# The last product of the down phase in two column halves, in a hybrid encoder layer on one Trainium2 core

## The chip, the core and the metric

The kernel runs on one core of a Trainium2 chip as one launch. A core has a matrix engine (TensorE, PE in the profile, with its weight loads as PEld), a vector engine (VectorE, DVE), a scalar engine (ScalarE, ACT), a general engine (GpSimd, POOL) and a queue that mostly issues transfers (SyncE, SP). Each works through its own instructions in order; semaphores order work between engines. Working memory on the core is SBUF, and matrix products land in PSUM, which here is handed out as tiles of 128 partitions x 512 fp32 values, eight of them, in two rings of four (`mm` and `hy`). Arrays live in HBM and move by DMA.

The metric is the device time of one execution, in microseconds (us), as the median over runs.

## The reference, cut to what matters

The layer has a convolution and recurrence stage, an attention stage and a feed-forward stage; only the last one and the final norm matter here:

```
def _rms_norm(x, g):
    xf = x.astype(jnp.float32)
    y = xf * lax.rsqrt(jnp.mean(xf * xf, axis=-1, keepdims=True) + EPS)
    return (y * g.astype(jnp.float32)).astype(x.dtype)
...
        h = h + jnp.square(jax.nn.relu(_rms_norm(h, norm_ff_g[l]) @ ff_w1[l])) @ ff_w2[l]
    return _rms_norm(h, final_norm_g)
```

There is one such layer. `h` has 2048 rows of 1024 columns, `ff_w1` is 1024 x 4096 and `ff_w2` 4096 x 1024, all in fp32. A row's root needs the squares of all its 1024 columns, so the two column halves of a row come together before it can be scaled and stored.

## The kernel before, in words

**Products in three passes.** An fp32 operand is split into a high and a low part (`halves`, L1622 and L1623, or L365), and `mm3` makes a product of three matmuls: high x high (L354), high x low (L357), low x high (L358). A "pass" below is one such matmul instruction.

**The down phase.** The second matrix product of the feed-forward stage is made by a Strassen-like scheme of 2 x 2 blocks: seven products `i` in the order `ORDER_DOWN = (1, 6, 7, 5, 3, 2, 4)` for each quarter `o` of the 4096 inner columns, 28 products in all. Each product is made for two groups `tp` of 512 activation rows, and over four steps `k` of 128 inner values. One step is four blocks `m` of 128 columns of the product's output times three passes of 512 columns (the 512 rows of the group: the result lies transposed, output features on partitions). After step `k == 3` the four PSUM tiles (`bank[m]`, from the ring `mm` for `tp` 0 and `hy` for `tp` 1) are added to accumulators `acc[i, tp]` in SBUF by DVE (L1949).

**The way out.** When a quarter-block of the result is complete, it is turned back: `turn` (L1879) makes four transposes of 128 x 128 on TensorE (L1882) into one PSUM tile, takes the sum of squares on ACT (L1884) into `ss`, and multiplies the tile by the final gain on DVE (L1885). `finish(c, dst)` (L1887) does the rest for 512 rows `c`: on DVE the mean of squares of both column halves (`mo`, L1891), a root by nine more small instructions after a first guess (`rsqrt`, L229 to L233), then scaling by the root, for even `c` the right column half on DVE (L1897) and the left half on ACT (L1899), and a store after every second block of 128 rows (L1902; 256 rows x 512 columns, 512 KB; the right half on SP's queue, the left half on ACT's). The functions wait in a list `outs`, from which the step loop takes one or two after each step's passes, and what is left is run after the loop. The last product (number 27, `i` = 4, `tp` = 1) completes rows 1024 to 1535 (`c` = 2). While it is made, the list holds the four turns and the `finish` of rows 0 to 511 (`c` = 0), whose last block was completed by the product just before.

**What sets the order.** The framework decides the order of the instructions on each engine when the program is built, by a simulated timeline, taking what was traced first where several are ready. It also places all semaphores. `keep_in_program_order` pins one instruction behind whatever was traced last before it on its engine; in this part it is used for the four adds of the last product alone (L1951).

Of the kernel before, what the change touches and what calls it, by code (L numbers as in the profile page):

```python
# [10 lines left out]
F32 = mybir.dt.float32  # L11
# [3 lines left out]
ALU = mybir.AluOpType  # L15
# [5 lines left out]
D = 1024  # L21
# [112 lines left out]
class Prog:  # L134
# [1592 lines left out]
    def ffn(self):  # L1727
        nc, tc, a = self.nc, self.tc, self.a
# [4 lines left out]
        prods = [(o, i) for o in range(4) for i in self.ORDER_DOWN]  # L1733
        down = [(n, tp, k) for n in range(len(prods)) for tp in range(2) for k in range(4)]
        aq, bq = {}, {}
# [37 lines left out]
        with tc.tile_pool(name="up", bufs=1) as U:  # L1773
# [25 lines left out]
            us, cs = {}, {}  # L1799
            for n, (tp, g, i) in enumerate(steps):  # L1800
# [13 lines left out]
                if n + 2 >= len(steps):  # L1814
                    k = n + 2 - len(steps)
# [4 lines left out]
                bank = self.ffn_product(wq.pop(0), i) if n > 1 else self.first[n]  # L1820
                u, c = us.setdefault(g, {}), cs.setdefault(g, {})
# [14 lines left out]
                else:  # L1836
# [5 lines left out]
                    t = [self.stage() for _ in range(4)]  # L1842
# [12 lines left out]
        with tc.tile_pool(name="down", bufs=1) as B:  # L1855
            acc, ms = {}, []
            on = [B.tile([128, D], F32, tag="on", name="on", bufs=2) for _ in range(2)]
            for tp in range(2):
                for h in range(2):
                    v = on[tp][:, 512 * h:512 * h + 512]  # L1860
# [8 lines left out]
            def residual(i, tp, k):  # L1869
                n, h = {2: (0, 0), 7: (1, 1), 3: (1, 0), 4: (0, 1)}[i]  # L1870
                v = acc[i, tp][:, k]
                nc.sync.dma_start(out=v, in_=h2[2 * tp + n, :, 4 * h + k])
                nc.gpsimd.tensor_tensor(v, v, ms[2 * tp + n], ALU.mult)
                if i == 4:
                    nc.gpsimd.tensor_tensor(v, v, acc[7, tp][:, k], ALU.subtract)

            ss = B.tile([128, 4, 2, 4], F32, name="ss")

            def turn(c, h, src, dst, t, tag):  # L1879
                pt = self.ps.tile([128, 512], F32, tag=tag, name=tag, bufs=4)  # L1880
                for k in range(4):
                    nc.tensor.transpose(pt[:, 128 * k:128 * k + 128], src[:, k, 128 * t:128 * t + 128], self.ident)  # L1882
                junk = B.tile([128, 512], F32, tag="junk", name="junk", bufs=1)
                nc.scalar.activation(junk, pt, AF.Square, accum_out=ss[:, c, h, t:t + 1])  # L1884
                nc.vector.tensor_tensor(dst[:, t], pt, gl[:, 512 * h:512 * h + 512], ALU.mult)  # L1885

            def finish(c, dst):  # L1887
                m = B.tile([128, 4], F32, tag="mo", name="mo", bufs=2)
                q = self.rbp[:, 4 * c:4 * c + 4]
                for h in range(2):  # L1890
                    nc.vector.scalar_tensor_tensor(m, ss[:, c, h], 1.0 / D, m if h else q, ALU.mult, ALU.add)  # L1891
                rv = self.rsqrt(B, m, "or")
                for t in range(4):
                    for h in range(2):
                        v = dst[h][:, t]
                        if h and c % 2 == 0:
                            nc.vector.tensor_scalar(v, v, rv[:, t:t + 1], None, ALU.mult)  # L1897
                        else:
                            nc.scalar.mul(v, v, rv[:, t:t + 1])  # L1899
                        if t % 2:  # L1900
                            r0 = 512 * c + 128 * (t - 1)
                            (nc.sync if h and c % 2 == 0 else nc.scalar).dma_start(  # L1902
                                out=self.out[r0:r0 + 256, 512 * h:512 * h + 512].rearrange("(t p) c -> p t c", p=128),
                                in_=dst[h][:, t - 1:t + 1])
# [8 lines left out]
            def add(i, j, tp, eng):  # L1913
                for m in range(4):
                    eng.tensor_tensor(acc[i, tp][:, m], acc[i, tp][:, m], acc[j, tp][:, m], ALU.add)

            early = [(i, tp, k) for i in (7, 4, 3, 2) for tp in range(2) for k in range(4)]
            outs = []
            V, G = nc.vector, nc.gpsimd
            for s, (n, tp, k) in enumerate(down):  # L1920
                o, i = prods[n]
                if n == 0 and tp == 0:
                    sums_w(k, nc.vector.tensor_tensor)
                if s + 3 < len(down):
                    fetch_b(s + 3, G if s > 199 and k else V)
                if o < 3 and tp == 0 and i == 2:
                    load_w(o + 1, k)
                if o < 3 and tp == 0 and i == 4:
                    sums_w(k, late=True)
                if early and (3 < s < 20 or s > 19 and s % 3):  # L1930
                    residual(*early.pop(0))
                if k == 0:
                    bank = [self.hy() if tp else self.mm() for _ in range(4)]
                (ah, al), (bh, bl) = aq[n, k], bq.pop(s)
                for m in range(4):
                    msl = slice(128 * m, 128 * m + 128)
                    self.mm3(bank[m], ah[:, msl], al[:, msl], bh, bl, k == 0, k == 3)
                if tp and n + 1 < len(prods):
                    fetch_a(n + 1, k)
                for _ in range(min(len(outs), 2 if len(outs) > 4 or n + 1 == len(prods) else 1)):  # L1940
                    outs.pop(0)("mm" if tp else "hy")
                if k < 3:
                    continue
                for m in range(4):
                    v = acc[i, tp][:, m]
                    if o == 0 and i in (1, 6, 5):
                        nc.scalar.copy(v, bank[m])
                    else:
                        d = nc.vector.tensor_tensor(v, bank[m], v, ALU.add)  # L1949
                        if s + 1 == len(down):  # L1950
                            tc.keep_in_program_order(d)  # L1951
                if o < 3:
                    continue
                if i == 1:
                    add(2, 1, tp, G)
                elif i == 6:
                    add(6, 1, tp, V)
                elif i == 7:
                    add(7, 6, tp, V)
                    add(3, 6, tp, G)  # L1960
                elif i == 5:
                    add(3, 5, tp, V)
                    add(5, 7, tp, G)
                    add(4, 7, tp, G)
                    if tp:
                        outs += turned(1, 0, 1, 5, 1)
                elif i == 3:
                    c = 2 * tp + 1
                    if not tp:
                        outs += turned(3, 1, 1, 5, 1)  # L1970
                    outs += turned(c, tp, 0, 3, 6, (acc[6, tp], acc[1, tp]))
                elif i == 2:
                    outs += turned(2 * tp, tp, 0, 2, 7)
                elif i == 4:
                    outs += turned(2 * tp, tp, 1, 4, 5, (acc[7, tp], acc[5, tp]))
            for x in outs:
                x("mm")


TC_ARGS = dict(schedule_with_timeline_sim=True)  # L1980
# [123 lines left out]
```

## Time and profile before

| | |
|---|---|
| three runs | 3126.7, 3130.87 and 3132.18 us, median 3130.87 |
| profiled execution | 3127.22 us, its span 3125.4 us |
| granted clock of TensorE over the span | 0.987 of full speed |
| busy share of the span | PE 97%, DVE 63%, ACT 48%, POOL 37% |
| the last product, from its first pass to the start of its last | 3094.96 to 3107.43 us |
| busy from 3100 us to the end, in us of 26 | PE 10.26, DVE 14.67, ACT 10.63 |
| last store issued | 3119.37 us |

The span runs from the first to the last instruction of the profiled execution. A timeline row gives start, duration, engine, line of the kernel, operation, output and inputs with their sizes, the count of instructions merged in it and, in brackets, how long the engine had stood idle and which instruction released it. A matmul's duration includes its way through the array; the next one starts before it ends, so its price is the distance of two starts.

### The profile page before, as it was taken

How to read it: one execution, taken by the hardware profiler on the slowest of the kernel's cores; microseconds unless marked ns; L12 is line 12 of the kernel's file. 1: busy time of each engine (PE TensorE's matmuls, PEld its weight loads, DVE VectorE, ACT ScalarE, POOL GpSimd, SP SyncE). 2: the span in 40 equal slices, each digit the busy share in tenths (PEclk: the TensorE clock that was granted, in tenths of full speed). 3: DMA queues.
4: the chain of work that ended last, by engine and by line, in shares of the span. 5: the costliest groups of instructions: out<-in, count | busy, mean ns of one | idle time of the engine just before them, and what ended most of it. 6: DMA issues, size and time to landing. Idle time of an engine off the chain costs nothing.

```text
span 3125.4 us, 42916 instructions
## 1 busy us (share of the span) xinstructions
PE 3031.2 (97%) x14257; PEld 2377.4 (76%) x14257; DVE 1960.3 (63%) x3448; ACT 1487.1 (48%) x2907; POOL 1146.5 (37%) x802
## 2 busy tenths in 40 slices
PE   8999999989999898999999999999999999999998
PEld 6655667766677666888888888888888888888876
DVE  7965466446646455777765556557555686565695
ACT  5443366533656225555544455556555443333335
POOL 0122012200113343324141327776565475242693
PEclk9999999999999998999999999999999999999999
DMA  6564767676877897455385647656644565353524
GB/s 211 153 212 163 235 204 220 192 217 217 240 207 246 267 315 242 142 184 197 115 280 175 226 154 246 207 187 219 213 151 150 167 216 187 111 165 112 161 91 172
DMA packets 444101, 607.07 MB, mean 194 GB/s; under 512 B 38494, under 2 KB 248542, under 8 KB 442856
## 3 DMA queue, kind: packets, MB, share of 16 engines
q1 hardware_dynamic: 405988, 546.54, 54.5%
q10 hardware_dynamic: 37892, 57.79, 5.4%
q8 instruction: 113, 1.85, 0.2%
q14 instruction: 108, 0.88, 0.1%
HBM read 401.79 MB, written 202.41 MB: 193 GB/s over the span
## 4 chain that ended last, share of the span: by engine, by line
PE 84%; DMA 6%; DVE 4%; ACT 2%; issue 2%; POOL 1%; SPq 0%; ACTq 0%; DVEq 0%; POOLq 0%
PE mm L354 17%; PE mm L358 17%; PE mm L357 17%; PE hy L358 6%; PE hy L354 6%; PE hy L357 6%; PE hy L177 3%; PE mm L912 2%; PE hy L943 2%; PE hy L985 1%; DMA a<-hy 1%; PE hy L1279 1%; PE mm L674 1%; PE mm L703 1%; PE hy L1281 1%
## 5 line engine op out<-in xcount | busy, mean ns | idle before, releaser
L1623 DVE TENSOR_TENSOR bl<-wr,bh 128x512 fp32r<-128x512 f32 x213 | 240.3, 1134 | 129.9 <-ACT bh L1622 129.7
L1622 ACT CAST ah<-w 128x512 fp32r<-128x512 f32 x284 | 176.6, 623 | 301.5 <-PE hy L357 155.2
L365 DVE TENSOR_TENSOR wl<-wn,wh 128x512 fp32r<-128x512 f32 (+1 forms) x300 | 218.1, 773 | 99.9 <-ACT wh L365 99.4
L354 PE MATMUL mm<-xh,wh 128*128 128x512 f32 x640 | 267.5, 419 | 12.1 <-ACT wh L365 9.1
L990 POOL TENSOR_TENSOR b<-b,a 128x512 f32<-128x512 f32 x64 | 87.4, 1367 | 509.3 <-ACT b L988 214.5
L357 PE MATMUL mm<-xl,wh 128*128 128x512 f32 x640 | 255.6, 399 | 0.7 <-DVE xl L365 0.6
L358 PE MATMUL mm<-xh,wl 128*128 128x512 f32 x640 | 254.8, 399 | 0.0
L1622 ACT CAST bh<-wr 128x512 fp32r<-128x512 f32 x232 | 143.5, 621 | 229.1 <-PE mm L358 177.0
L1623 DVE TENSOR_TENSOR al<-w,ah 128x512 fp32r<-128x512 f32 x236 | 216.7, 918 | 55.4 <-ACT ah L1622 55.2
L358 PE MATMUL mm<-bh,al 128*128 128x512 f32 x576 | 224.0, 391 | 2.6 <-POOL al L1623 2.6
L354 PE MATMUL mm<-bh,ah 128*128 128x512 f32 x576 | 225.9, 392 | 0.4 <-DVE acc L1785 0.3
L357 PE MATMUL mm<-bl,ah 128*128 128x512 f32 x576 | 224.9, 390 | 0.0
L365 ACT CAST wh<-wn 128x512 fp32r<-128x512 f32 (+1 forms) x300 | 166.6, 618 | 113.8 <-PE mm L358 51.4
L357 PE MATMUL mm<-act,wh 128*128 128x512 f32 x512 | 200.5, 393 | 0.8 <-DVE act L365 0.8
L354 PE MATMUL mm<-act,wh 128*128 128x512 f32 x512 | 198.8, 394 | 2.5 <-ACT wh L365 2.4
L358 PE MATMUL mm<-act,wl 128*128 128x512 f32 x512 | 199.1, 392 | 0.0
L354 PE MATMUL hy<-bh,ah 128*128 128x512 f32 x448 | 175.2, 391 | 0.0
L357 PE MATMUL hy<-bl,ah 128*128 128x512 f32 x448 | 174.6, 390 | 0.0
L358 PE MATMUL hy<-bh,al 128*128 128x512 f32 x448 | 174.4, 390 | 0.0
L354 PEld LDWEIGHTS mm<-xh,wh 128*128 128x128 f32 x640 | 121.3, 190 | 67.2 <-issue 19.0
L354 PE MATMUL mm<-wh,xh 128*128 128x256 f32 (+1 forms) x512 | 155.9, 305 | 10.6 <-ACT xh L365 8.1
L336 POOL TENSOR_TENSOR b<-b 128x512 f32<-128x512 f32 x32 | 58.3, 1822 | 277.4 <-DVE b L333 137.6
(369 smaller groups left out, 8282.3 us busy)
## 6 DMA issues: line engine op xcount, KB each, us to landing
wr<-hc SPq DMA_DIRECT2D x224, 256.0 KB
w<-in_ff_w_dram SPq DMA_DIRECT2D x172, 256.0 KB
hc<-wn SPq DMA_DIRECT2D x128, 256.0 KB
wn<-in_w_in_dram SPq DMA_DIRECT2D x100, 256.0 KB
hc<-q SPq DMA_DIRECT2D x96, 256.0 KB
fs<-a SPq DMA_DIRECT2D x32, 512.0 KB
a<-fs SPq DMA_DIRECT2D x64, 256.0 KB
a<-zs SPq DMA_DIRECT2D x64, 256.0 KB
```

Source lines behind the costliest of these rows:

```text
L177: b = self.nc.tensor.matmul(*products[-1], start=True, stop=True)
L336: nc.gpsimd.tensor_tensor(e[1], f, b, ALU.subtract)
L354: first = mm(ps, lh, rh, start=start, stop=False)
L357: mm(ps, lh, rl, start=False, stop=False)
L358: self.last = mm(ps, ll, rh, start=False, stop=stop)
L365: both = (self.nc.scalar.copy(hi, src), self.nc.vector.tensor_tensor(lo, src, hi.bitcast(F32), ALU.subtract))
L674: mul(p[:, m], w[:, k, ms], mt[k // 4][:, k % 4], start=k == 0, stop=k == 7)
L912: nc.tensor.matmul(pp, dm[:, m], t[:, m], start=True, stop=True)
L943: nc.tensor.matmul(pg, em[:, m], y, start=True, stop=True)
L990: nc.gpsimd.tensor_tensor(xt, xt, hi[:, m], ALU.mult)
L1622: self.nc.scalar.copy(hi, src)
L1623: eng.tensor_tensor(lo, src, hi.bitcast(F32), ALU.subtract)
```

## The change

The last product for `tp` = 1 leaves the step loop and is made by a new function, `last_block`: twice the four steps, first for the columns 0 to 255 of the four PSUM tiles (activation rows 1024 to 1279), then for the columns 256 to 511 (rows 1280 to 1535) of the same four tiles. After each half, four adds of 256 columns bring it to the accumulator, each pinned in program order, and two turns and a `finish` for these two blocks of 128 rows go on the list. `finish` gets a range of blocks for that. In the first half two entries of the list are taken after each step; in the second half none after step 0 and one after each later step. What is left is run at the end.

```diff
@@ -1884,19 +1884,20 @@
                 nc.scalar.activation(junk, pt, AF.Square, accum_out=ss[:, c, h, t:t + 1])
                 nc.vector.tensor_tensor(dst[:, t], pt, gl[:, 512 * h:512 * h + 512], ALU.mult)
 
-            def finish(c, dst):
-                m = B.tile([128, 4], F32, tag="mo", name="mo", bufs=2)
-                q = self.rbp[:, 4 * c:4 * c + 4]
+            def finish(c, dst, ts=range(4)):
+                m = B.tile([128, 4], F32, tag="mo", name="mo", bufs=2)[:, 0:len(ts)]
+                t0 = ts[0]
+                q = self.rbp[:, 4 * c + t0:4 * c + t0 + len(ts)]
                 for h in range(2):
-                    nc.vector.scalar_tensor_tensor(m, ss[:, c, h], 1.0 / D, m if h else q, ALU.mult, ALU.add)
+                    nc.vector.scalar_tensor_tensor(m, ss[:, c, h, t0:t0 + len(ts)], 1.0 / D, m if h else q, ALU.mult, ALU.add)
                 rv = self.rsqrt(B, m, "or")
-                for t in range(4):
+                for t in ts:
                     for h in range(2):
                         v = dst[h][:, t]
                         if h and c % 2 == 0:
-                            nc.vector.tensor_scalar(v, v, rv[:, t:t + 1], None, ALU.mult)
+                            nc.vector.tensor_scalar(v, v, rv[:, t - t0:t - t0 + 1], None, ALU.mult)
                         else:
-                            nc.scalar.mul(v, v, rv[:, t:t + 1])
+                            nc.scalar.mul(v, v, rv[:, t - t0:t - t0 + 1])
                         if t % 2:
                             r0 = 512 * c + 128 * (t - 1)
                             (nc.sync if h and c % 2 == 0 else nc.scalar).dma_start(
@@ -1913,6 +1914,28 @@
             def add(i, j, tp, eng):
                 for m in range(4):
                     eng.tensor_tensor(acc[i, tp][:, m], acc[i, tp][:, m], acc[j, tp][:, m], ALU.add)
+
+            def last_block(i, tp):
+                n = len(prods) - 1
+                bank = [self.hy() for _ in range(4)]
+                for half in range(2):
+                    cs = slice(256 * half, 256 * half + 256)
+                    for k in range(4):
+                        (ah, al), (bh, bl) = aq[n, k], bq[len(down) - 4 + k]
+                        for m in range(4):
+                            msl = slice(128 * m, 128 * m + 128)
+                            self.mm3(bank[m][:, cs], ah[:, msl], al[:, msl], bh[:, cs], bl[:, cs], k == 0, k == 3)
+                        for _ in range(min(len(outs), 1 if half and k else 0 if half else 2)):
+                            outs.pop(0)("mm")
+                    for m in range(4):
+                        v = acc[i, tp][:, m, cs]
+                        tc.keep_in_program_order(nc.vector.tensor_tensor(v, bank[m][:, cs], v, ALU.add))
+                    c = 2 * tp
+                    for t in (2 * half, 2 * half + 1):
+                        outs.append(lambda tag, t=t: turn(c, tp, acc[i, tp], acc[5, tp], t, tag))
+                    outs.append(lambda tag, half=half: finish(c, (acc[7, tp], acc[5, tp]), range(2 * half, 2 * half + 2)))
+                for x in outs:
+                    x("mm")
 
             early = [(i, tp, k) for i in (7, 4, 3, 2) for tp in range(2) for k in range(4)]
             outs = []
@@ -1929,6 +1952,10 @@
                     sums_w(k, late=True)
                 if early and (3 < s < 20 or s > 19 and s % 3):
                     residual(*early.pop(0))
+                if s + 4 >= len(down):
+                    if k == 3:
+                        last_block(i, tp)
+                    continue
                 if k == 0:
                     bank = [self.hy() if tp else self.mm() for _ in range(4)]
                 (ah, al), (bh, bl) = aq[n, k], bq.pop(s)
@@ -1946,9 +1973,7 @@
                     if o == 0 and i in (1, 6, 5):
                         nc.scalar.copy(v, bank[m])
                     else:
-                        d = nc.vector.tensor_tensor(v, bank[m], v, ALU.add)
-                        if s + 1 == len(down):
-                            tc.keep_in_program_order(d)
+                        nc.vector.tensor_tensor(v, bank[m], v, ALU.add)
                 if o < 3:
                     continue
                 if i == 1:
@@ -1973,8 +1998,6 @@
                     outs += turned(2 * tp, tp, 0, 2, 7)
                 elif i == 4:
                     outs += turned(2 * tp, tp, 1, 4, 5, (acc[7, tp], acc[5, tp]))
-            for x in outs:
-                x("mm")
 
 
 TC_ARGS = dict(schedule_with_timeline_sim=True)
```

## The prediction

> **What bounds the kernel now.** I read the head of the page and its chain first, then the same chain cut to the last 30 us, then the timeline of that stretch on all engines.
>
> ```profile
> span 3125.4 us, 42916 instructions
> PE 84%; DMA 6%; DVE 4%; ACT 2%; issue 2%; POOL 1%; SPq 0%; ACTq 0%; DVEq 0%; POOLq 0%
> ```
> ```profile
> 3106.65 1.67 DVE acc L1897 x4
> 3108.32 0.61 DVE acc L1949
> 3108.97 2.14 PE mm L1882 x13
> ```
>
> TensorE bounds the kernel as a whole, but not its end. The chain near the end runs over DVE: the four scalings of `finish(0)` (L1897; it norms rows 0 to 511 of the output), then the adds of the last product (L1949), then its transposes. The change touches only the last 31 us, so the timeline of these gives the rest (start, duration, engine, line):
>
> ```profile
> 3094.96 0.39 PE L354 MATMUL hy<-bh,ah 128*128 128x512 f32 x1
> ...
> 3099.50 0.28 PE L1882 MATMUL mm<-ident,acc 128*128 128x128 f32 x1
> ...
> 3101.30 1.04 PE L1882 MATMUL mm<-ident,acc 128*128 128x128 f32 x8
> ...
> 3101.71 2.85 DVE L1885 TENSOR_TENSOR acc<-mm,gl 128x512 f32<-128x512 f32 x4 [4.30 <-ACT junk L1884]
> ...
> 3104.03 0.39 PE L358 MATMUL hy<-bh,al 128*128 128x512 f32 x1
> ...
> 3106.65 1.67 DVE L1897 TENSOR_SCALAR acc<-acc,or_y 128x512 f32<-128x512 f32 x4
> ...
> 3107.43 0.39 PE L358 MATMUL hy<-bh,al 128*128 128x512 f32 x1
> ...
> 3108.24 2.48 DVE L1949 TENSOR_TENSOR acc<-hy,acc 128x512 f32<-128x512 f32 x4
> ...
> 3108.97 2.45 PE L1882 MATMUL mm<-ident,acc 128*128 128x128 f32 x16 [1.16 <-DVE acc L1949]
> ...
> 3110.77 0.42 PEld L1882 LDWEIGHTS mm<-ident,acc 128*128 128x128 f32 x4 [0.18 <-DVE acc L1949]
> 3111.14 0.60 ACT L1884 ACTIVATE junk<-mm 128x512 f32<-128x512 f32 x1 [1.92 <-PE mm L1882]
> ...
> 3111.86 2.85 DVE L1885 TENSOR_TENSOR acc<-mm,gl 128x512 f32<-128x512 f32 x4 [1.14 <-ACT junk L1884]
> ...
> 3113.30 0.60 ACT L1884 ACTIVATE junk<-mm 128x512 f32<-128x512 f32 x1
> ...
> 3114.62 0.15 DVE L1891 SCALAR_TENSOR_TENSOR mo<-ss,mo 128x4 f32<-128x4 f32 x1
> ...
> 3116.78 1.67 DVE L1897 TENSOR_SCALAR acc<-acc,or_y 128x512 f32<-128x512 f32 x4
> ...
> 3118.14 0.38 ACTq L1902 DMA_DIRECT2D out_dram<-acc  x1
> ...
> 3119.37 0.38 ACTq L1902 DMA_DIRECT2D out_dram<-acc  x1
> ```
>
> The last pass starts at 3107.43, but DVE is inside `finish(0)` from 3101.71 to 3108.24: that, not TensorE, starts the last chain. Four adds, sixteen transposes, four squares, four gains, the root (3114.62 to 3116.78, 2.16 us of 4-column instructions), scalings, stores.
>
> **The change, part by part.** *Passes.* 48 passes of 512 columns become 96 of 256. From 3104.03 to 3107.43 lie 15 steps of 512 columns, 0.227 us each. For 256 columns:
>
> ```profile
> 1029.85 0.28 PE L354 MATMUL mm<-wh,xh 128*128 128x256 f32 x1
> ...
> 1032.96 0.28 PE L358 MATMUL mm<-wh,xl 128*128 128x256 f32 x1
> ```
>
> 26 steps in 3.11 us, 0.120 each, with a weight load before each of them as in the new passes. So 96 x 0.120 - 48 x 0.227 = +0.6 us of TensorE. A transpose paces at (1.04 - 0.27) / 7 = 0.11 (the row at 3101.30). The first half is 48 x 0.120 + 16 x 0.11 (the four turns of rows 0 to 511, popped after its steps 0 and 1) = 7.5 us: from 3094.96 to 3102.5. The same sum for the old block, 47 x 0.227 + 16 x 0.11 = 12.4, meets its 3107.43 - 3094.96.
>
> *What the tail counts.* Transposes, squares, gains, scalings (16, 4, 4, 8) and stores (4, two on SP's queue with those of rows 0 to 511, two on ACT's) stay as many; the adds become 8 of half the width; a second `mo` pair and root (12 instructions at 0.2 us) are added. A store's issue holds ACT 0.38 us, as before.
>
> *Where the first half's adds go.* They are pinned behind whatever was traced last on DVE, and that is the last L1897 of `finish(0)`; the old adds had the same pin and started at 3108.24 on its heels. The transposes of `finish(0)` stood after 20 passes (3099.50); as 40 half passes that is 4.8 in place of 4.5 us, so +0.25: the adds start at 3108.5. Bounds: -0.5 if they come some passes earlier, +0.8 if later. Nothing covers this: DVE is busy until then.
>
> *A wait for the bank.* Both halves of one block write the same PSUM tile, columns 0-255 and 256-511. Does a pass to the second columns wait for an add that reads the first? No row shows that pair; the nearest is a tile whose columns 0-255 ACT reads and whose columns 256-271 DVE reads:
>
> ```profile
> 513.72 0.38 ACT L851 ACTIVATE st<-mm 128x256 f32<-128x256 f32 x1
> 514.14 0.18 DVE L856 TENSOR_TENSOR sg<-mm,par 128x16 f32<-128x16 f32 x1 [1.16 <-ACT st L851]
> ...
>   ACT st L851: 18.9, 9
> ```
>
> DVE had no datum to wait for and still stood 18.9 us in 9 waits until ACT left the tile. So access is ordered by tile, not by column, and I take the wait as there: TensorE stands from 3102.5 until the first add is done. Behind the waiting pass on TensorE's queue are all passes of the second half and, between them, the transposes of the first half's turns; for those wait ACT's squares, DVE's gains and the first half's root. The price lies between 0 (columns apart, passes start at 3102.5) and 6.5 us of standing. The Trainium skill (PSUM — Partial Sum Buffer, "PSUM bank collisions raise a hardware error") says the same of writes: two engines on one bank collide whichever columns they touch, so software keeps them apart by bank; the trace agrees for two readers, and by this rule the sum is the one with the wait.
>
> An add of 256 columns has no row either. The 512-column one paces at (2.48 - 0.68) / 3 = 0.60 us; half of that, 0.30, is the floor, 0.60 the ceiling. A copy of 258 columns from PSUM:
>
> ```profile
> L1156 DVE COPY cb<-hy 128x258 f32<-128x258 f32 x2 | 0.8, 422 | 0.0
> ```
>
> I take 0.43 for one and a pace of 0.36. The passes restart at 3108.5 + 0.43 + 0.05 = 3109.0; the other three banks come free in time (three passes take 0.36).
>
> *The clock.* TensorE now stands over 6 us. Granted clock by the microsecond (third number from the end of a row; the first pair after the time is TensorE's busy time):
>
> ```profile
> 37.00:38.00 1.00, 0.62 (x1) 0.30 (x2) 0.33 (x2) 0.00 (x0) 0.00 (x0) 0.90 0.00 0
> ...
> 44.00:45.00 1.00, 1.00 (x4) 0.79 (x3) 0.97 (x2) 0.00 (x0) 0.00 (x0) 0.68 0.00 0
> ```
> ```profile
> 1079.72 6.44 PE L691 MATMUL mm<-kt,wm 128*128 128x256 f32 x15 [10.94 <-ACT o L681]
> ```
> ```profile
> 1085.00:1086.00 1.00, 1.00 (x4) 0.85 (x3) 0.79 (x5) 1.00 (x5) 0.00 (x0) 0.65 1.03 398
> ```
> ```profile
> 3113.00:3114.00 1.00, 0.00 (x0) 0.00 (x0) 0.96 (x2) 0.95 (x4) 0.00 (x0) 0.61 0.73 281
> ```
> ```profile
> 680.98 0.43 PE L357 MATMUL mm<-wl,xh 128*128 128x272 f32 x1
> ...
> 682.57 0.43 PE L357 MATMUL mm<-wl,xh 128*128 128x272 f32 x1
> ...
> 684.97 0.29 PE L358 MATMUL mm<-wh,xl 128*128 128x272 f32 x1
> ...
> 685.98 0.29 PE L357 MATMUL mm<-wl,xh 128*128 128x272 f32 x1
> ```
>
> The last transposes end at 3111.4 and the clock halves at 3113.2 (0.61 is 22% of 1.0 and the rest 0.5): 1.8 us of standing are enough. It comes back 5.9 us after a restart (1079.72 to 1085.7) and 7.2 us after another (37.4 to 44.6). At half clock 272 columns pace at 1.59 / 7 = 0.227, later at 1.01 / 8 = 0.126: 1.8 times. Those 5.9 and 7.2 us include breaks, the new passes have none, so I take 5.1 slow us, which cost 5.1 x (1 - 0.126 / 0.227) = 2.3; bounds 0 (no fall) and 3.2 (7.2 us). The Trainium skill (TensorE: Matmul & The Clock Gate, "What's actually happening") gives a free-running window of 3413 ns, one idle window for the fall and one busy one for the return. By 3.4 slow us the term would be 1.5, an estimate, and the sum 0.8 lower; the trace agrees on fall and return, and its returns took longer.
>
> *The first half's chain.* `turn` of block 0 is popped after the second half's step 1 and block 1 after step 2, so the second stands behind 36 passes and 8 transposes: 36 x 0.120 + 8 x 0.11 + 2.3 = 7.5 us, to 3116.5. The square starts 0.37 after the last transpose's issue (3110.77 to 3111.14), at 3116.7, gain +0.72, `mo` +0.60, root +2.16, two L1897 at (3108.24 - 3106.65) / 4 = 0.40 each: 3121.0. The last adds are pinned behind those. The passes, done by 3118.5, no longer count.
>
> *The second half's chain.* Last add starts 3 x 0.36 later, +0.43 + 0.05 + 0.37 to the first square, 3122.9; at half clock (TensorE stood 3 us again) +0.2: 3123.1. Second square, its gain, `mo`, root: 0.72 + 0.72 + 0.60 + 2.16: the root is ready at 3127.3, against 3116.78. What halving saves in this last chain is two squares (1.4 us) and 1.0 us of adds (1.08 for 3 x 0.60, and the narrower last one); what it costs is that a whole first chain, with a root of its own, now stands in line between `finish(0)` and it.
>
> *Stores.* Before, 2.1 MB leave at the end; now the last half has 1.05 MB, the first half's is gone 7 us before.
>
> ```profile
> 3118.00:3119.00 1.00, 0.00 (x0) 0.00 (x0) 0.46 (x2) 1.00 (x3) 0.00 (x0) 0.50 0.43 168
> ...
> 3123.00:3124.00 1.00, 0.00 (x0) 0.00 (x0) 0.00 (x0) 0.00 (x0) 0.00 (x0) 0.50 0.84 324
> ```
>
> Bytes flow from 3118.6 to 3123.8 (168 and 324 at some 405 GB/s); 1.05 MB need 2.6 us of the 5.2. Gain 2.6, since the second store is issued in time.
>
> Sum: 3127.3 - 3116.8 - 2.6 = **+7.9 us**. The profiled execution took 3127.22 us around its span of 3125.4, within the shown runs (median 3130.87), so on the median: 3138.8.
>
> **The rivals.** *No wait for the bank.* For it: the columns are apart; against: L856. Passes run on from 3102.5 to 3108.3, both turns follow the adds at once, first square 3110.4, root 3114.6, last adds 3115.4, first square 3117.3, root 3121.5: +4.7 - 2.6 = +2.1, 3133.0. *Wait, but full clock.* Against it: 1.8 us sufficed at 3113.2. 7.9 - 2.3 - 0.2 = +5.4, 3136.3. *Worse order.* If the half's turns end up behind all 48 passes, 12 more at up to 0.215 lie ahead of the chain (+1.4 to +2.6): about +10, 3140.9. *Not slower:* DVE takes the first half's adds ahead of `finish(0)` and the half's chain is through before the last pass. Last pass by 3094.96 + 96 x 0.120 + 24 x 0.11 = 3109.1, last add, transposes and first square 0.85 later, root 4.2 after that at 3114.2: -2.6 - 2.6 = -5.2, 3125.7. It decides in its favour only if those adds start by 3101, and `finish(0)` holds DVE from 3101.71 with 6.5 us of work; from 3104 on it is no gain.
>
> **How the numbers follow.** Forecast 0.58 (its own spread +6 to +9.5), no bank wait 0.13, full clock 0.12, worse order 0.11, not slower 0.06. Range 3132 to 3143: it leaves out the last rival and the tails of two others. 0.2% (about what a measurement of this kernel can tell from no change) is 6.3 us: the forecast lies over it for the most part, the two middle rivals under it, and even -5.2 does not reach it downward. Slower 0.66, same 0.31, faster 0.03.
>
> **What would show it.** TensorE standing from about 3102.5 to 3109 with the release by the DVE add; granted clock 0.50 in the second half's first passes; the half's L1897 right ahead of the last adds; two roots in line after `finish(0)`; 1 MB in the last store. It is wrong if the second half's passes start at 3102.5, or if the first half's adds start before L1897 of `finish(0)`.

## The result, and the profile after

| | before | after |
|---|---|---|
| median of the runs made together, 22 of each | 3127.73 us (3123.55 to 3133.09) | 3134.32 us (3130.26 to 3141.6) |
| profiled execution, its span | 3127.22 us, 3125.4 us | 3137.81 us, 3136.1 us |
| first pass of the last product | 3094.96 us | 3100.13 us |
| tail: from that pass to the end of the span | 30.4 us | 36.0 us |
| granted clock of TensorE over the span | 0.987 | 0.986 |

The changed kernel is slower: ratio 1.0022, 95% interval 1.0016 to 1.0028, or 6.6 us between the medians. The two profiled executions differ by more, but 5.2 us of that had already passed when the last product began. But for one small `mo` instruction of the new part on DVE (3095.01), all instructions ahead of it stand in the same order on every engine in both programs, so that part is a difference between executions, and the comparison goes by the tail: +5.5 us here. A second profiled execution of the same kernel (further down) gave a tail of 37.3, +6.9.

The timeline of the changed kernel's tail (start, duration, engine, line, in brackets the idle time before and who ended it). L1898 is the old L1897, L1932 the adds of `last_block`, and L1976 those of the product before, which completes rows 0 to 511:

```profile
3100.11 2.47 DVE L1976 TENSOR_TENSOR acc<-mm,acc 128x512 f32<-128x512 f32 x4
3100.13 0.28 PE L354 MATMUL hy<-bh,ah 128*128 128x256 f32 x1
...
3102.65 0.27 PE L1882 MATMUL mm<-ident,acc 128*128 128x128 f32 x1
...
3105.56 2.85 DVE L1885 TENSOR_TENSOR acc<-mm,gl 128x512 f32<-128x512 f32 x4 [2.97 <-ACT junk L1884]
...
3107.50 0.28 PE L358 MATMUL hy<-bh,al 128*128 128x256 f32 x1
...
3110.48 1.68 DVE L1898 TENSOR_SCALAR acc<-acc,or_y 128x512 f32<-128x512 f32 x4
3112.07 1.41 DVE L1932 TENSOR_TENSOR acc<-hy,acc 128x256 f32<-128x256 f32 x4
3112.55 0.58 PE L354 MATMUL hy<-bh,ah 128*128 128x256 f32 x1 [4.77 <-DVE acc L1932]
...
3119.20 0.49 PE L1882 MATMUL mm<-ident,acc 128*128 128x128 f32 x3
3119.79 0.60 ACT L1884 ACTIVATE junk<-mm 128x512 f32<-128x512 f32 x1 [0.79 <-PE mm L1882]
...
3120.49 0.28 PE L358 MATMUL hy<-bh,al 128*128 128x256 f32 x1
...
3123.27 0.88 DVE L1898 TENSOR_SCALAR acc<-acc,or_y 128x512 f32<-128x512 f32 x2
3124.07 1.41 DVE L1932 TENSOR_TENSOR acc<-hy,acc 128x256 f32<-128x256 f32 x4
3124.63 1.43 PE L1882 MATMUL mm<-ident,acc 128*128 128x128 f32 x8 [3.87 <-DVE acc L1932]
...
3125.90 0.60 ACT L1884 ACTIVATE junk<-mm 128x512 f32<-128x512 f32 x1 [1.30 <-PE mm L1882]
...
3130.10 0.88 DVE L1898 TENSOR_SCALAR acc<-acc,or_y 128x512 f32<-128x512 f32 x2
```

Read it from the top. The first half's last pass starts at 3107.50, and the next pass on TensorE starts 5.05 us later, released by the first add. That add could not start before DVE had left `finish(0)`, whose four scalings (3110.48) end as the adds begin. Then the second half's passes run to 3120.49, but the last adds do not follow them: they come at 3124.07, right behind the first half's two scalings, and TensorE stands again, 3.87 us, until the first of them is done. The last scalings start at 3130.10, 6.0 us before the end; before, they started at 3116.78, 8.6 us before it.

The chain that ended last says the same (start, length, what): scalings, add, passes; and again scalings and add.

```profile
3110.52 1.64 DVE acc L1898 x4
3112.16 0.34 DVE acc L1932
3112.55 0.58 PE hy L354
...
3123.27 0.88 DVE acc L1898 x2
3124.15 0.34 DVE acc L1932
```

The same kernel by the microsecond (length, then busy time of PE, PEld, DVE, ACT and POOL, granted clock, DMA share, GB/s):

```profile
3112.00:3113.00 1.00, 0.45 (x2) 0.45 (x3) 1.00 (x4) 1.00 (x2) 0.00 (x0) 0.55 0.72 268
...
3115.00:3116.00 1.00, 1.00 (x9) 1.00 (x8) 0.00 (x0) 0.00 (x0) 0.00 (x0) 0.74 1.06 412
...
3125.00:3126.00 1.00, 1.00 (x7) 0.48 (x6) 0.48 (x2) 0.10 (x1) 0.00 (x0) 0.88 0.96 371
...
3131.00:3132.00 1.00, 0.00 (x0) 0.00 (x0) 0.00 (x0) 0.43 (x1) 0.00 (x0) 0.50 0.10 39
...
3134.00:3135.00 1.00, 0.00 (x0) 0.00 (x0) 0.00 (x0) 0.00 (x0) 0.00 (x0) 0.50 0.54 207
```

A mean of 0.55 between full and half clock puts the fall at 3112.10; 0.74 puts the return at 3115.52. TensorE restarted at 3112.55, so 3.0 us of its passes ran slow. The last store's bytes flow from 3131.9 to 3134.5, 2.6 us against 5.2 before.

### The profile page after: what moved, and what is told of

It reads as the page before. It is cut to its first block, busy times and chain, and to the rows that moved or that the text cites. A ratio compares the mean times of both kernels' runs of the same rounds, so it can differ in the third digit from the quotient of the medians.

```text
span 3136.1 us, 43028 instructions
## 1 busy us (share of the span) xinstructions
PE 3034.9 (97%) x14305; PEld 2383.6 (76%) x14305; DVE 1963.0 (63%) x3464; ACT 1486.1 (47%) x2907; POOL 1145.6 (37%) x802
## 4 chain that ended last, share of the span: by engine, by line
PE 84%; DMA 6%; DVE 4%; ACT 2%; issue 2%; POOL 1%; SPq 0%; ACTq 0%; DVEq 0%; POOLq 0%
PE mm L354 17%; PE mm L358 17%; PE mm L357 17%; PE hy L354 6%; PE hy L358 6%; PE hy L357 6%; PE hy L177 3%; PE mm L912 2%; DMA a<-hy 2%; PE hy L943 2%; PE hy L985 1%; PE mm L703 1%; PE hy L1279 1%; PE mm L674 1%; PE hy L1154 1%
## 5 line engine op out<-in xcount | busy, mean ns | idle before, releaser
L354 PE MATMUL hy<-bh,ah 128*128 128x512 f32 (+1 forms) x464 | 179.1, 386 | 4.8 <-DVE acc L1932 4.8
L357 PE MATMUL hy<-bl,ah 128*128 128x512 f32 (+1 forms) x464 | 178.0, 384 | 0.0
L358 PE MATMUL hy<-bh,al 128*128 128x512 f32 (+1 forms) x464 | 177.5, 383 | 0.0
```

The source lines that it names most:

```text
L354: first = mm(ps, lh, rh, start=start, stop=False)
L357: mm(ps, lh, rl, start=False, stop=False)
L358: self.last = mm(ps, ll, rh, start=False, stop=stop)
```

## The experiments

The theory: the two pins cost the time, each in its place. The first holds the first half's adds behind `finish(0)`, for which TensorE stands and its clock falls; the second puts the first half's whole chain ahead of the last adds. Without both, halving is worth a few us. The rivals were that the narrow passes, the second root or the two stores cost it. Every kernel ran beside the kernel before.

| kernel | first pass, span, us | tail, us | ratio to before, 95% |
|---|---|---|---|
| before | 3094.96, 3125.4 | 30.4 | |
| after | 3100.13, 3136.1 | 36.0 | 1.0022 (1.0016 to 1.0028) |
| after, once more | 3097.30, 3134.6 | 37.3 | one run |
| second half in PSUM tiles of its own | 3094.58, 3126.2 | 31.6 | 1.0003 (0.9994 to 1.0012) |
| TensorE kept busy between the halves | 3095.49, 3130.6 | 35.1 | 1.0012 (1.0003 to 1.0020) |
| only the passes halved | 3093.15, 3122.7 | 29.6 | 0.9997 (0.9988 to 1.0007) |
| one `finish` for both halves | 3101.38, 3137.6 | 36.2 | 1.0015 (1.0003 to 1.0028) |
| only the first half's adds pinned | 3091.30, 3126.1 | 34.8 | 1.0009 (1.0000 to 1.0018) |
| only the second half's adds pinned | 3095.34, 3126.6 | 31.3 | 1.0003 (0.9993 to 1.0013) |
| no pins | 3098.54, 3126.4 | 27.9 | 0.9997 (0.9988 to 1.0005) |
| no pins, again | 3095.06, 3122.9 | 27.8 | 0.9991 (0.9982 to 1.0000) |
| kernel before, no pins | 3094.53, 3124.9 | 30.4 | 1.0004 (0.9995 to 1.0013) |
| no pins, rows 0 to 511 scaled on GpSimd: right half | 3102.62, 3130.6 | 28.0 | 0.9994 (0.9986 to 1.0003) |
| the same, left half | 3093.78, 3122.0 | 28.2 | 0.9997 (0.9987 to 1.0007) |

Single tails are told apart where they differ by more than the 1.3 us between the two executions of the changed kernel; the two without pins agree to 0.1. Most ratios alone can't be told from 1.

**The wait for the bank: PSUM tiles of its own for the second half.** The adds and pins stay.

```diff
-                bank = [self.hy() for _ in range(4)]
                 for half in range(2):
+                    bank = [self.mm() if half else self.hy() for _ in range(4)]
...
-                            outs.pop(0)("mm")
+                            outs.pop(0)("hy" if half else "mm")
...
```

> The second half of the last product gets four PSUM tiles of its own (the ring of the turns), the turns of the first half go to the ring that the first half leaves; all else as changed. 'Tail' is the time from the first pass of the last product to the end of the span: 30.4 us before, 36.0 us changed. Theory (the wait for the tile of the first half costs, by holding the passes and with them the first half's turns): the second half's passes start when the first half's end, 7.5 to 8.5 us after the product's start in place of 12.4, the clock stays at 1.0, the turns of the first half follow its adds at once; tail about 31, 5 us under the changed kernel. Rival (the two roots and the pinned adds in line on DVE cost, the passes would have been hidden): the passes move up, but the tail stays at 35 to 36.

The timeline of this kernel, first pass, first pass of the second half, first adds:

```profile
3094.58 0.28 PE L354 MATMUL hy<-bh,ah 128*128 128x256 f32 x1
...
3102.06 0.28 PE L354 MATMUL mm<-bh,ah 128*128 128x256 f32 x1
...
3106.51 1.41 DVE L1932 TENSOR_TENSOR acc<-hy,acc 128x256 f32<-128x256 f32 x4
```

The second half's passes start 0.12 us behind the first half's last one, while the adds still come 11.9 us after the first pass, as in the changed kernel. So TensorE waited for the shared tile and for nothing else. The wait stands in the program as a semaphore that the framework placed; whether the chip needs it for columns apart, no run here shows. The wait with the slow clock behind it was worth 36.0 - 31.6 = 4.4 us, or 5.7 by the other execution.

**The clock: TensorE kept busy while it waits.** Forty transposes into a PSUM tile that nobody reads; they are work on top.

```diff
+                    if half:
+                        pt = self.mm()
+                        for j in range(40):
+                            d = nc.tensor.transpose(pt[:, 0:128], gl[:, 0:128], self.ident)
+                            if j == 0:
+                                tc.keep_in_program_order(d)
```

> As changed, with 40 transposes of a constant (4.4 us) between the halves' passes, so that TensorE does not stand; they write a PSUM tile that nobody reads. Theory (the halved clock costs): granted clock 1.0 in the second half's passes, about 15 passes at 0.12 in place of 0.21 us, tail 34.6 in place of 36.0. Rival (the slow passes are covered by DVE): tail 36.0. If the transposes run past the first add, up to 0.5 is lost again.

The timeline, the forty and the first pass behind them, and a window behind that pass (the third number from the end is the clock):

```profile
3102.98 4.53 PE L1926 MATMUL mm<-ident,gl 128*128 128x128 f32 x40
...
3107.91 0.39 PE L354 MATMUL hy<-bh,ah 128*128 128x256 f32 x1 [0.41 <-DVE acc L1938]
```
```profile
3108.00:3109.00 1.00, 1.00 (x9) 1.00 (x10) 0.85 (x3) 0.41 (x1) 0.00 (x0) 1.00 1.02 379
```

The restart lies 12.42 us after the first pass, exactly as in the changed kernel; only the clock is full behind it. The tail is 35.1: 0.9 and 2.2 below the two executions of the changed kernel. The slow clock explains that much and no more; the wait remains.

**The changed kernel once more**, for the spread of that term.

> The changed kernel a second time, for the time that the clock stays halved. Theory (the clock is set on a free-running grid, so the slow stretch after a restart differs by run): TensorE restarts 12.4 us after the product's start again; the slow stretch, 3.0 us in the first profile, lies somewhere between 3 and 7 us; tail 36 to 37.5. Rival (fixed in the program): 3.0 us again, tail 36.0.

Its timeline, and below it its windows with TensorE alone (length, busy, clock, DMA share, GB/s):

```profile
3109.71 0.58 PE L354 MATMUL hy<-bh,ah 128*128 128x256 f32 x1 [4.77 <-DVE acc L1932]
...
3122.64 1.94 PE L1882 MATMUL mm<-ident,acc 128*128 128x128 f32 x8 [3.86 <-DVE acc L1932]
```
```profile
3107.00:3108.00 1.00, 0.00 (x0) 0.89 0.00 0
...
3114.00:3115.00 1.00, 1.00 (x8) 0.69 0.73 281
```

The restart again comes 12.41 us after the first pass. The clock fell at 3107.78 and came back at 3114.62, so 4.9 us after the restart ran slow instead of 3.0, and the last eight transposes took 1.94 instead of 1.43 us. At 0.213 us for a slow pass (four steps from 3112.93 to 3113.78 in the changed kernel) against 0.120, 1.9 us more of slow clock cost 1.9 x (1 - 0.120 / 0.213) = 0.8; with the 0.5 of the transposes that is the 1.3 us between the two tails.

**Is it the narrow passes?** The passes halved, then the four old adds of 512 columns and one `finish`, as before. The adds stay pinned.

```diff
-                    for m in range(4):
-                        v = acc[i, tp][:, m, cs]
...
+                for m in range(4):
+                    v = acc[i, tp][:, m]
+                    tc.keep_in_program_order(nc.vector.tensor_tensor(v, bank[m], v, ALU.add))
+                outs.extend(turned(2 * tp, tp, 1, 4, 5, (acc[7, tp], acc[5, tp])))
```

> Only the passes are halved in width: both halves' 96 passes, then four adds of 512 columns, four turns and one finish as before. Theory (TensorE is not what starts the last chain; the transposes of rows 0 to 511 stand after 21 half-width passes, so finish(0) comes 1.3 us earlier, as in the changed kernel): the last add ends with the last pass, at 14.3 us after the product's start in place of 15.8; tail 29.0 in place of 30.4. Rival (the passes cost what they add, 0.6 us): tail 31.0.

The four adds in the timeline of this kernel:

```profile
3105.52 2.48 DVE L1932 TENSOR_TENSOR acc<-hy,acc 128x512 f32<-128x512 f32 x4 [0.34 <-PE hy L358]
```

They wait for the last pass, not for DVE, and come 12.4 us after the first pass, against 13.28 before. The passes alone cost nothing; the tail is 0.9 us shorter, as much as the adds come earlier.

**Is it the second root or the stores?** One `finish` for all four blocks at the end, the rest as in the changed kernel.

```diff
-                    outs.append(lambda tag, half=half: finish(c, (acc[7, tp], acc[5, tp]), range(2 * half, 2 * half + 2)))
+                outs.append(lambda tag: finish(c, (acc[7, tp], acc[5, tp])))
```

> As changed, with no finish after the first half: one root, one scaling and one set of stores for all four blocks at the end. Theory (the first half's root and scalings, 3.0 us, stand in line before the last adds, and the halved store gives 2.6 back): the last adds start 3 us earlier, the end keeps the store of 2 MB; tail 35.6 against 36.0. Rival (the first half's root is covered by the passes): last adds start at the same time, tail 38.6.

Its timeline, and its windows with TensorE alone:

```profile
3113.80 0.58 PE L354 MATMUL hy<-bh,ah 128*128 128x256 f32 x1 [4.77 <-DVE acc L1932]
...
3122.88 1.41 DVE L1932 TENSOR_TENSOR acc<-hy,acc 128x256 f32<-128x256 f32 x4
```
```profile
3111.00:3112.00 1.00, 0.00 (x0) 0.58 0.00 0
...
3117.00:3118.00 1.00, 1.00 (x6) 0.51 1.06 410
```

The last adds come 21.5 us after the first pass instead of 23.9, since no root and no scalings stand ahead of them. The tail is the same 36.2: its last scalings start at 3128.97, 8.6 us before the end, so the 2.6 us of the halved last store are lost again. So what the second root costs ahead of the last adds (2.4 us) and what the split stores save (2.6 us) balance each other, and the two together do not make the loss.

**Which pin?** First neither, then each alone.

```diff
-                        tc.keep_in_program_order(nc.vector.tensor_tensor(v, bank[m][:, cs], v, ALU.add))
+                        nc.vector.tensor_tensor(v, bank[m][:, cs], v, ALU.add)
```

> As changed, without the pins on the adds of the last product; in the built order the first half's adds then stand among the gains of rows 0 to 511, ahead of their root. Theory (the pin behind the scalings of rows 0 to 511 makes the wait): the first half's adds run near 7 to 9 us after the product's start in place of 12, TensorE stands under 1.5 us, the clock stays, tail 27 to 29, under that of before (30.4). Rival (the DVE work of three groups in line sets the end): tail 31 or more. The second half's adds stand ahead of the first half's gains in this order, so DVE may wait for passes: that would show as idle time of DVE before L1932.

The timeline without pins:

```profile
3098.54 0.28 PE L354 MATMUL hy<-bh,ah 128*128 128x256 f32 x1
...
3105.29 0.41 DVE L1932 TENSOR_TENSOR acc<-hy,acc 128x256 f32<-128x256 f32 x1
...
3112.13 1.14 DVE L1932 TENSOR_TENSOR acc<-hy,acc 128x256 f32<-128x256 f32 x3 [0.41 <-PE hy L358]
...
3112.52 0.57 ACT L1884 ACTIVATE junk<-mm 128x512 f32<-128x512 f32 x1
...
3117.81 1.95 ACT L1900 ACTIVATE acc<-acc,or_y 128x512 f32<-128x512 f32 x3 [2.47 <-DVE or_y L233]
```

The first half's adds now start at +6.75 us, between the gains of rows 0 to 511. TensorE doesn't stand at all. One add of the second half comes early (3107.95); the last three wait for the last passes alone, from +13.6 us on. The same kernel was run again.

> The changed kernel without both pins once more, for a narrower interval against the kernel before: tail 27.9 against 30.4, so 2.5 us or 0.08% faster (0.9992) by theory; 1.0000 or more if the shorter tail is lost elsewhere.

It gave 27.8. The first pin alone:

```diff
-                        tc.keep_in_program_order(nc.vector.tensor_tensor(v, bank[m][:, cs], v, ALU.add))
+                        d = nc.vector.tensor_tensor(v, bank[m][:, cs], v, ALU.add)
+                        if not half:
+                            tc.keep_in_program_order(d)
```

> As changed, with the pin on the first half's adds alone; the second half's adds are free and stand in the built order right behind the first half's. Theory (the first pin makes TensorE stand and the clock fall, and that is the larger part of the loss): first add 12 us after the product's start, TensorE stands 4.8 us, clock 0.50 after it, as changed; the last adds come with the last passes, ahead of the first half's root; both roots end together; tail 34 to 35, 2 us under the changed kernel (36.0 and 37.3). Rival (the second pin, the first half's root in line, is the larger part): tail under 31.5.

Its timeline, and its windows with TensorE alone:

```profile
3103.71 0.58 PE L354 MATMUL hy<-bh,ah 128*128 128x256 f32 x1 [4.76 <-DVE acc L1932]
```
```profile
3102.00:3103.00 1.00, 0.00 (x0) 0.60 0.00 0
...
3109.00:3110.00 1.00, 1.00 (x10) 0.99 0.00 0
```

All of the standing is there, with 5.3 us of slow clock behind it: 34.8, so the first pin costs 34.8 - 27.9 = 6.9. The second alone (`if half:` in the same place):

> As changed, without the pin on the first half's adds alone; the second half's adds stay pinned behind the first half's scalings. Theory (of the two pins the first makes TensorE stand, the second puts the first half's root ahead of the last adds): TensorE does not stand between the halves, clock 1.0, the last adds start about 17.5 us after the product's start in place of 23.9; tail 29 to 30, some 1 to 2 us over the kernel without both pins (27.9). Rival (the second pin is the one that costs): tail over 34.

Its timeline, with the last scaling of rows 0 to 511, the first square of the first half and the last adds:

```profile
3108.51 0.71 ACT L1900 ACTIVATE acc<-acc,or_y 128x512 f32<-128x512 f32 x1
3109.12 0.57 ACT L1884 ACTIVATE junk<-mm 128x512 f32<-128x512 f32 x1
...
3114.09 1.41 DVE L1932 TENSOR_TENSOR acc<-hy,acc 128x256 f32<-128x256 f32 x4
```

No standing between the halves here, and yet 31.3, over the 29 to 30 expected. The timeline shows what the expectation left out: the first half's squares wait behind ACT's scalings of rows 0 to 511, so its chain is late, and the pinned last adds with it (+18.75 instead of the +13.6 of the last three without pins). This pin costs 3.4 alone, and 1.2 to 2.5 on top of the first.

**Is it the pin, whatever the width?** The kernel before without its four pins, all else as it was.

```diff
-                        if s + 1 == len(down):
-                            tc.keep_in_program_order(d)
```

> The kernel before without its pins on the last four adds; in the built order the adds stand inside the root of rows 0 to 511. Theory (what holds the end of the kernel before is finish(0) ahead of the adds on DVE): the adds end at the last pass plus 0.7, squares start 2 us earlier than before, tail 28.4 in place of 30.4. Rival (the passes or the adds in wait hold the root): tail 30 to 31.

Its timeline, with the first add of the last product, the last scaling of rows 0 to 511 on ACT and the first square of the last product:

```profile
3105.39 0.69 DVE L1949 TENSOR_TENSOR acc<-hy,acc 128x512 f32<-128x512 f32 x1
...
3110.09 0.70 ACT L1899 ACTIVATE acc<-acc,or_y 128x512 f32<-128x512 f32 x1
3110.70 0.57 ACT L1884 ACTIVATE junk<-mm 128x512 f32<-128x512 f32 x1
```

The expectation fell. The adds do move forward, by 2.4 us, into the root of rows 0 to 511, but they stretch that root, so ACT's scalings of these rows end later too, and the first square of the last product stands right behind them on ACT. It comes at 3110.70 - 3094.53 = 16.2 us after the first pass, and 3111.14 - 3094.96 = 16.2 it was before. The tail is the same 30.4. So the 2.5 us that the kernel without pins gains over before come with the halving, and not from the missing pins alone.

**More than that?** Without pins both halves end together: four left scalings follow each other (three from 3117.81, the fourth at 3119.66), all 2.1 MB leave after them, and the end comes 8.6 us behind the last root, as before, not 6.0. The first half's squares (3112.52) had waited behind ACT's scalings of rows 0 to 511. Two kernels moved half of these scalings to GpSimd and popped the turns one step earlier, first the right half (DVE's).

```diff
-                            nc.vector.tensor_scalar(v, v, rv[:, t - t0:t - t0 + 1], None, ALU.mult)
+                            (nc.vector if c else nc.gpsimd).tensor_scalar(v, v, rv[:, t - t0:t - t0 + 1], None, ALU.mult)
...
-                        for _ in range(min(len(outs), 1 if half and k else 0 if half else 2)):
+                        for _ in range(min(len(outs), 1 if half and k else 2)):
```

> Without both pins, the four right-half scalings of rows 0 to 511 on GpSimd in place of DVE, and the first half's turns one step earlier. Theory (with the wait gone, DVE's work in line sets the end): DVE is 1.6 us emptier, the last adds wait for the passes alone; tail 26.5 to 27.5 against 27.9 without pins. Rival (GpSimd's scalings delay DVE, or the last passes set the end): tail 28 or more.

Its timeline, with DVE's scalings of the first and of the second half:

```profile
3121.88 0.88 DVE L1898 TENSOR_SCALAR acc<-acc,or_y 128x512 f32<-128x512 f32 x2
...
3124.64 0.88 DVE L1898 TENSOR_SCALAR acc<-acc,or_y 128x512 f32<-128x512 f32 x2
```

Missed: 28.0. The stores are staggered now and the end comes 6.0 behind the last scalings' start (3124.64), but the two roots ran one after the other, 2.76 us apart, which eats the 2.6. Then the left half (ACT's), with a third buffer for the root and the stores of rows 0 to 511 all on SP's queue.

```diff
...
+                        elif c == 0:
+                            nc.gpsimd.tensor_scalar(v, v, rv[:, t - t0:t - t0 + 1], None, ALU.mult)
...
-                            (nc.sync if h and c % 2 == 0 else nc.scalar).dma_start(
+                            (nc.sync if c == 0 or h and c % 2 == 0 else nc.scalar).dma_start(
...
```

> No pins at all; the left half of rows 0 to 511 is scaled on GpSimd instead of ScalarE, its stores go on SP's queue, the turns of the first half are popped one step earlier, and the root has a third buffer so that it need not wait for GpSimd's reads. In the version without pins the first half's squares stood behind ScalarE's four scalings of rows 0 to 511, so both halves were scaled together and 2.1 MB still left at the end: the end came 8.6 us after the last root, where the pinned kernel needs 6.0. If that is what holds the rest, the first half's squares now run before the last pass, its root is through ahead of the second half's, its 1 MB leaves earlier, and the tail (first pass of the last product to the end of the span) is 25.5 to 27 us against 27.9 without pins. Rival: GpSimd's four scalings (6.2 us in an earlier run) push the stores of rows 0 to 511 back until they fill the gap, or the two roots again end together; then the tail stays at 27.5 to 28.5. Either way the time is within 0.2% of the kernel before.

Its timeline, with the scalings of rows 0 to 511 on both engines and the first of the last three adds:

```profile
3105.29 2.46 DVE L1898 TENSOR_SCALAR acc<-acc,or_y 128x512 f32<-128x512 f32 x4
3105.35 6.89 POOL L1900 TENSOR_SCALAR acc<-acc,or_y 128x512 f32<-128x512 f32 x4 [12.07 <-DVE or_y L233]
...
3108.26 0.41 DVE L1934 TENSOR_TENSOR acc<-hy,acc 128x256 f32<-128x256 f32 x1
```

The tail is the rival's: 28.2. GpSimd needs 6.9 us for its four scalings, DVE's four beside them take 2.46 instead of 1.67, a gain of the first half (3107.67) now stands ahead of the last three adds (L1934 here), and these come 14.5 us after the first pass instead of 13.6. The scalings of the two halves start only 2.0 us apart (3113.39 and 3115.35). How much each of these costs was not measured. Nothing tried went below 27.8. The version without pins is the best of them, 0.9997 and 0.9991 of before: clearly faster than the changed kernel, not clearly told from the kernel before.

## Why the prediction was right, and where its sizes were off

The direction and the mechanism held: +7.9 us was forecast, +6.6 measured between the medians, +5.5 and +6.9 in the tails. The time itself, 3138.8 forecast and 3134.32 measured, was off by 4.5 us; 3.1 of these are the median before, which was taken from three runs (3130.87) and came out at 3127.73 over 22. By its steps, in us from the first pass of the last product:

| step | predicted | after |
|---|---|---|
| first half's adds start | 13.5 | 11.9 |
| TensorE restarts | 14.0 | 12.4 |
| square of the half's second block | 21.7 | 19.7 |
| last adds start | 26.0 | 23.9 |
| first square of the last half | 28.1 | 25.8 |
| root ready | 32.3 | 30.0 |
| end | 38.3 | 36.0 |

- *Passes.* Right in pace: the second half's slow passes apart, they start 0.12 apart, and alone they cost nothing.
- *Where the first half's adds go.* The pin did what was said; the size failed. The step "as 40 half passes that is 4.8 in place of 4.5 us, so +0.25" took the transposes of rows 0 to 511 to keep their place in the amount of work. They came after 21 half passes (3102.65), at once when the adds of the product before were done (3100.11 and 2.47), so the gains of these rows start 5.4 us after the first pass, against 6.75 before, and the adds come 1.3 us earlier than before, not 0.25 later. It lay outside the bounds given, -0.5 to +0.8. This is the largest miss, 1.6 us. The lower end should have come from the datum: with steps half as long, the transposes could be handed out as early as their input was there. Why the order before left them until 3099.50, 2.1 us after their input (3094.95 and 2.47), no run shows.
- *The wait for the bank.* Right: TensorE stood until the first add was done, and with tiles of its own it did not. It stood 4.8 us instead of 6.5 only because the adds came earlier. The rival without a wait came to +2.1, a tail of 32.5; with tiles of its own it was 31.6.
- *The adds.* 0.41 us each at a pace of (1.41 - 0.41) / 3 = 0.33, for 0.43 and 0.36.
- *The clock.* It halved and came back as forecast, but 5.1 slow us were too many for the first execution (3.0, cost 1.3 instead of 2.3) and nearly right for the second (4.9). The last eight transposes were mostly at full clock in the first (1.43 us) and slow in the second (1.94); the 0.2 taken for them lies between.
- *The half's chain in line.* Right to the tenth: 3.5 us from the second square to the root, two scalings of 0.40, then the pinned adds.
- *The stores.* Right: 2.6 us of bytes, the end 6.0 us behind the root.
- *"Not slower".* Its condition, adds taken ahead of `finish(0)`, is nearly met by the kernel without pins: the first add starts at 6.75 us, among the gains, where the rival asked for 3101, 6.0 us after the first pass. There the root is ready 19.3 us after the first pass, as that rival had it, but only 2.5 of its 5.2 us came: it had counted the halved last store, and there both halves are stored together.

The sum of misses: 1.6 of the place of `finish(0)`, 1.0 of the clock and 0.3 of the last adds and transposes, less some 0.5 of smaller ones between the restart and the square (the second block's last transposes stand behind 39 passes, not 36), is about the 2.3 us between 38.3 and 36.0.

## What to carry to other kernels

Before splitting a product to overlap its two halves, look at what reads the first half and where that reader stands on its own queue: here the adds were pinned behind work of another part, the halves shared a PSUM tile, and the early half's result was late on both counts. A pin that cost nothing while it came last became the price of the change (36.0 or 37.3 against 27.9 us of tail). And count where the early half's later steps queue: even without pins its squares stood behind another part's scalings, so its store left right ahead of the last one (issued on ACT's queue at 3119.18 and 3120.40).

## What the hardware showed that I had not expected

TensorE's clock changed only on a fixed beat. Worked out from the means of the windows shown, the clock of the changed kernel fell at 3112.10, returned at 3115.52 and fell again at 3125.76: 3.42 and 3 x 3.41 us. The other three falls and returns lie two beats apart: 3107.78 and 3114.62, 3111.16 and 3117.98, 3102.20 and 3109.02 (6.84, 6.82, 6.82). What the beat asks for shows only in part. The window that held the restart ended the slow clock when TensorE was busy for 87% of it (from 3112.55), and didn't at 56% (restart 3103.71), 44% (3109.71) or 23% (3113.80); and the fall at 3125.76 followed a window that was busy for a third, since the transposes had run from 3124.63. The fall at 3111.16 (one `finish`) followed one that passes had filled to 38%, up to 3109.03. But the busy share of the records does not settle it: in the kernel before, by the rows at 37.00 and 44.00 that the prediction shows, the clock fell at 37.80 and came back at 44.64, two beats later, although TensorE was busy through the whole first beat. What else counts stays open. So after the standing between the halves the slow stretch had one beat or two, and the same program differs by 1.3 us between executions. The Trainium skill (TensorE: Matmul & The Clock Gate, "What's actually happening") gives free-running windows of 3413 ns; these runs agree on length and beat. It asks for an idle window before the fall, where here one that was a third busy sufficed. The prediction had read the 5.9 and 7.2 us of two other returns as a slower one. Counted from the fall they fit the same beat: the 7.2 us hold 0.4 us before 37.80 in which the clock was still full, and the 5.9 us end four beats after their fall (1072.04 to 1085.70, 13.66 us).
